# A drain instruction in GpSimd's stream at the start of the last gate pair

## The chip, the cores and the metric

The kernel runs on one core of a Trainium2 chip. The metric is the device time of one execution in microseconds (us), as the median over runs. Beside the timed runs there is one profiled execution, from which every duration below is read.

## The reference, cut to what matters

One layer of a streaming encoder trunk is computed for 2048 prompt frames and 32 sample frames of width 1024:

```python
def layer(h, p, conv_hist, pool_hist, pos, g_mix, w_in, conv_w, conv_b, pool_w, pool_scale,
          w_out, g_ple, w_ple_gate, w_ple):
    hn = rmsnorm(h, g_mix)
    proj = hn @ w_in
    ...
    h = h + jnp.concatenate([yA, yB], axis=-1) @ w_out
    gate = jax.nn.sigmoid(rmsnorm(h, g_ple) @ w_ple_gate)
    h = h + (p @ w_ple) * gate
    return h, new_conv, new_pool
```

After it a last RMSNorm with `g_final` is applied: `y = h * rsqrt(mean(h*h) + EPS) * g_final`. The change lies in the last stage, which computes the gate, the sum `h + (p @ w_ple) * gate` and the last RMSNorm.

## The kernel before, in words

Frames stand in tiles of 128; there are 16 tiles for the prompt (0 to 15) and a short one for the sample. The last stage takes the prompt's tiles in pairs (0 and 1, 2 and 3, up to 14 and 15). A pair's product with the gate weight is made of seven smaller products (`seven`), each of 12 matmuls, that add into three PSUM banks `x`, `y` and `z`. What comes out of a bank goes to `carry` (a copy by ScalarE) or to `out`.

For all pairs but the last, `out` and `done_g` finish a tile: the sigmoid on ScalarE, two VectorE operations (`L1584`, `L1585`), the sum of squares on ScalarE (`L94`, into `ssq_f`), then two operations of one column on GpSimd, `L73` (`ms_f`, mean and epsilon) and `L77` (`rstd_f`, the power -0.5), then VectorE's `L1592`, which multiplies the tile by `rstd_f` and `g_final`, and the DMA `L1593` that writes the tile out. From tile 6 on this DMA is issued by SyncE; for earlier tiles by GpSimd.

The last pair, tiles 14 and 15, is `last_pair`. It is called with a function `before` that finishes tile 13 in the middle of the pair (after the third of the seven products), by `done_g(13)`. Tile 12 has been finished by `done_g(12)` just ahead of the call. In `last_pair` the names are:

- `L1670`: VectorE adds what a PSUM bank holds to the carried half (`c_g`); `L1666`: ScalarE's sigmoid of it.
- `L1633` and `L1634` (`gated`): VectorE multiplies by the embedding product (`e`, or `e_l` from PSUM) and adds to `h`.
- `L1638` (`square`): ScalarE's sum of squares of a half; `L1641` and `L1643`: GpSimd adds the parts up; `L1650` (`root`): GpSimd's power -0.5 of the sum.
- `L1646` (`weigh`): the product with `g_final`, once on GpSimd (for the first half of tile 14), otherwise on VectorE.
- `L1657`, `L1659` (`normed`): VectorE and ScalarE multiply by the root, and the DMAs at `L1658` and `L1660` write out.
- `L1715`: the last product of the pair, in two halves of 256 columns, that adds into bank `x` after `L1670` has read it; `L109`: TensorE's embedding products `e_l`.

Every engine works its own instructions off in the order in which they stand. A scheduler places the instructions by dependencies and priorities; those marked by `fixed` (`keep_in_program_order`) stand where the program has them.

DMAs are issued from three places: SyncE (SP), ScalarE (ACT) and GpSimd (POOL). GpSimd issues 148 DMAs in all; the last are the writes of early tiles at `L1593`. At the kernel's end each engine has a drain instruction and all engines meet twice at a barrier, which GpSimd leads: it waits until the four others have arrived, then releases them. These instructions bear the line `L1845`, that of the kernel's call, and those at the start `L1836`.

Of the kernel before, what the change touches and what calls it, by code (L numbers as in the profile page):

```python
# [36 lines left out]
def trunk(ctx, tc, x_p, x_s, c_conv, c_pool, p_p, p_s, g_mix, w_in, conv_w, conv_b, pool_w,  # L37
          pool_scale, w_out, g_ple, w_gate, w_ple, g_fin, y_p, y_s, sc_p, sp_p, sc_s, sp_s):
    nc = tc.nc
# [16 lines left out]
    def bank(name):  # L56
        return ps_m.tile([P, 512], F32, tag="mm", name=name)
# [48 lines left out]
    def embed_product(ps, pps, wp, cs):  # L106
        for k in range(2):
            for q, (a, b) in enumerate(((0, 0), (0, 1), (1, 0))):
                nc.tensor.matmul(ps, pps[:, a, k], wp[k][b][:, cs], start=k + q == 0, stop=k == 1 and q == 2)  # L109
# [1194 lines left out]
    with ExitStack() as s2:  # L1304
# [308 lines left out]
        def last_pair(i, A, before):  # L1613
# [15 lines left out]
            fixed = lambda ins: tc.keep_in_program_order(ins)  # L1629
# [51 lines left out]
            def of_first(cs, eng):  # L1681
                square(0, cs)
                weigh(0, cs, eng)
# [8 lines left out]
            def rest():  # L1692
                of_first(cols_of(0), nc.gpsimd)

            def second(cols):

                ps = bank(f"e_l{cols.start}")[:, :cols.stop - cols.start]
                embed_product(ps, pps, wp, cols)
                return ps

            def upper_half():
                gated(1, cols_of(1), at_last["gate"], second(cols_of(1)))

            def end(X):

                t = st.tile([P, NH], F32, tag="t", name="g_l")
                m = NH // 2  # L1710
                cs = [slice(o, o + m) for o in (0, m)]
                for c, part in enumerate(cs):
                    for k in range(KH):
                        for a, b in FINE:
                            nc.tensor.matmul(X[:, part], A["22"][:, k, a], W["T4"][b][:, k, part], start=False,  # L1715
                                             stop=k == KH - 1 and (a, b) == FINE[-1], skip_group_check=True)
                    fixed(sigmoid(t[:, part], X[:, part], 1))
                    ee = second(part)
                    if c == 0:
                        normed(0, at_last["root"])  # L1720
                        square(1, cols_of(1))
                    gated(1, part, t[:, part], ee)
                    if c == 0:
                        weigh(1, cols_of(1))
                for part in cs:
                    square(1, part)
                weigh(1, cols_of(0))
                normed(1, root(1))
# [80 lines left out]
        for i in range(0, NT - 3, 2):  # L1809
# [8 lines left out]
            if i + 2 < NT - 3:  # L1818
                done_g(i + 1, h[1])
        last_pair(NT - 3, S[NT - 3], lambda: done_g(NT - 4, h[1], True))  # L1820

# [27 lines left out]
```

## Time and profile before

| what | us |
| --- | --- |
| median of the runs | 916.7 |
| runs | 914.71, 917.25, 916.7 |
| the profiled execution's own time | 913.25 |
| its span, from first to last instruction | 911.5 |

The profile's page gives the busy time of each engine: PE is TensorE's matmuls, PEld its weight loads, DVE is VectorE, ACT ScalarE, POOL GpSimd and SP SyncE. A letter q behind an engine's name is its sequencer: drains, semaphore waits and DMA issues are told of under that name and are not counted as busy. In a timeline the columns are the start in us, the duration in us, then engine, line, operation, the tile written and the tiles read, shape and count; in brackets stands the idle time of the engine ahead of it, and what ended it. The answer for one source line gives, for each kind of instruction of it, the count, the shortest, median and longest duration in ns, and the first and last start in us.

### The profile page before, as it was taken

The numbers are of one execution on the slowest core, as the hardware profiler recorded it, in microseconds if no ns is written. First come the engines' busy times: TensorE is split into PE (matmuls) and PEld (weight loads), VectorE is DVE, ScalarE is ACT, GpSimd is POOL, SyncE is SP. The second block draws the span as 40 slices with busy tenths as digits, with TensorE's granted clock in tenths as the row PEclk, the third lists the DMA queues.
The fourth block names the chain that finished last, engine by engine and source line by source line (L and its number), as shares of the span: only waits on it lengthen the run. The fifth ranks groups of instructions, "written<-read, shape, count | busy, mean of one in ns | idle before, by whom it ended". The sixth has DMA issues, their size and how long they took to land.

```text
span 911.5 us, 12171 instructions
## 1 busy us (share of the span) xinstructions
PE 894.6 (98%) x4174; PEld 722.5 (79%) x4174; DVE 702.9 (77%) x1158; ACT 460.6 (51%) x834; POOL 149.8 (16%) x290
## 2 busy tenths in 40 slices
PE   8999999999999999999999999999999999999996
PEld 6788888878888887877778887888788888778885
DVE  6899789797993697846667579965666988897885
ACT  7744555455443345533344366544434865565554
POOL 2210121222122114100000020121111211120012
PEclk9999999999999999999999999999999999999999
DMA  8255296748599767567746495887777975575554
GB/s 268 61 187 179 76 269 191 217 151 262 151 328 422 212 201 216 199 216 236 256 129 199 162 318 200 260 245 257 212 267 256 325 257 174 184 237 185 184 192 167
DMA packets 113387, 198.52 MB, mean 218 GB/s; under 512 B 13174, under 2 KB 70062, under 8 KB 112429
## 3 DMA queue, kind: packets, MB, share of 16 engines
q1 hardware_dynamic: 91309, 124.72, 42.5%
q0 software_dynamic: 19568, 68.62, 22.5%
q10 hardware_dynamic: 2448, 4.39, 1.3%
q8 instruction: 33, 0.54, 0.2%
q14 instruction: 29, 0.24, 0.1%
HBM read 132.53 MB, written 65.15 MB: 217 GB/s over the span
## 4 chain that ended last, share of the span: by engine, by line
PE 54%; issue 11%; DMA 10%; DVE 2%; POOL 1%; ACT 1%; POOLq 0%; ACTq 0%; DVEq 0%
PE x_g L185 9%; PE x_o L185 7%; PE z_g L185 5%; DMA raw_zab_0b<-in_w_in_dram 4%; PE x_zab L646 4%; PE x_zbv L646 3%; PE z_o L185 3%; PE x_ch L646 3%; PE y_g L185 2%; PE z_zab L646 2%; PE y_o L185 2%; DMA B<-p_d 2%; PE e L109 2%; PE z_ch L646 1%; PE z_zbv L646 1%
## 5 line engine op out<-in xcount | busy, mean ns | idle before, releaser
L185 PE MATMUL z_o<-wo,y_S 128*128 128x512 f32 x192 | 47.4, 389 | 0.0
L646 PE MATMUL x_zab<-B,w_zab_S 128*128 128x512 f32 x192 | 46.9, 393 | 0.4 <-DVE w_zab_S L84 0.2
L185 PE MATMUL x_o<-wo_T,y_S 128*128 128x512 f32 x192 | 46.3, 390 | 0.6 <-DVE c_o L1319 0.6
L185 PE MATMUL z_g<-wg,g_S 128*128 128x512 f32 x192 | 46.8, 391 | 0.0
L646 PE MATMUL z_zab<-B,w_zab_S 128*128 128x512 f32 x192 | 46.7, 391 | 0.0
L185 PE MATMUL x_o<-wo,y 128*128 128x512 f32 x192 | 45.2, 389 | 0.0
L646 PEld LDWEIGHTS x_zab<-B,w_zab_S 128*128 128x128 f32 x192 | 35.7, 188 | 9.4 <-DVE w_zab_S L84 0.6
L185 PEld LDWEIGHTS x_o<-wo_T,y_S 128*128 128x128 f32 x192 | 35.9, 188 | 8.4 <-DVE c_o L1319 1.0
L185 PEld LDWEIGHTS x_o<-wo,y 128*128 128x128 f32 x192 | 36.1, 188 | 7.7
L646 PEld LDWEIGHTS z_zab<-B,w_zab_S 128*128 128x128 f32 x192 | 35.8, 188 | 7.8 <-DVE w_zab_S L84 0.3
L185 PEld LDWEIGHTS z_o<-wo,y_S 128*128 128x128 f32 x192 | 36.1, 188 | 7.5
L646 PE MATMUL x_ch<-B,w_ch_S 128*128 128x512 f32 x168 | 41.9, 392 | 0.0
L185 PEld LDWEIGHTS z_g<-wg,g_S 128*128 128x128 f32 x192 | 35.8, 188 | 7.5 <-ACT c_g L1573 0.2
L646 PE MATMUL z_ch<-B,w_ch_S 128*128 128x512 f32 x168 | 40.5, 390 | 1.1 <-ACT U L986 1.1
L646 PE MATMUL x_zbv<-B,w_zbv_S 128*128 128x512 f32 x168 | 40.9, 392 | 0.3 <-ACT zs L986 0.3
L646 PE MATMUL z_zbv<-B,w_zbv_S 128*128 128x512 f32 x168 | 40.4, 390 | 0.0
L646 PEld LDWEIGHTS z_ch<-B,w_ch_S 128*128 128x128 f32 x168 | 31.5, 188 | 8.1 <-ACT U L986 1.6
L646 PEld LDWEIGHTS x_zbv<-B,w_zbv_S 128*128 128x128 f32 x168 | 31.3, 188 | 8.1 <-ACT zs L986 0.8
L646 PEld LDWEIGHTS x_ch<-B,w_ch_S 128*128 128x128 f32 x168 | 31.3, 188 | 7.3 <-ACT U L986 0.4
L646 PEld LDWEIGHTS z_zbv<-B,w_zbv_S 128*128 128x128 f32 x168 | 31.5, 188 | 6.5
L81 ACT CAST y_S<-y_fS 128x512 fp32r<-128x512 f32 x28 | 17.0, 619 | 28.1 <-PE x_o L185 12.2
L1319 DVE TENSOR_TENSOR c_o<-x_o,x 128x512 f32<-128x512 f32 x14 | 9.7, 689 | 22.6 <-PE x_o L185 22.6
(552 smaller groups left out, 2285.0 us busy)
## 6 DMA issues: line engine op xcount, KB each, us to landing
wn<-in_w_in_dram SPq DMA_DIRECT2D x24, 512.0 KB, 4.7
y<-y_d SPq DMA_DIRECT2D x16, 512.0 KB, 6.5
p_dT<-T POOLq DMA_DIRECT2D x15, 512.0 KB, 5.2
e<-e_d SPq DMA_DIRECT2D x15, 512.0 KB, 5.0
x<-in_x_prompt_dram SPq DMA_DIRECT2D x14, 512.0 KB, 4.9
B<-p_d POOLq DMA_DIRECT2D x3, 2048.0 KB, 16.8
B<-p_dT POOLq DMA_DIRECT2D x3, 2048.0 KB, 22.8
h_d<-x SPq DMA_DIRECT2D x12, 512.0 KB, 6.3
```

Of the source, the lines that this page charges most:

```text
L81: ins = nc.scalar.copy(hi, src)
L109: nc.tensor.matmul(ps, pps[:, a, k], wp[k][b][:, cs], start=k + q == 0, stop=k == 1 and q == 2)
L185: nc.tensor.matmul(ps[:n], lhs[:, k, a, :n], w[b][:, k], start=start and k + q == 0, stop=k == KH - 1 and q == 2, skip_group_check=True)
L646: nc.tensor.matmul(ps, lhs[:, k, x], b[:, k, y], start=start and k + q == 0, stop=stop and k == KH - 1 and q == 2, skip_group_check=True)
L1319: add = lambda o, a, b: nc.vector.tensor_tensor(o, a, b, op=ALU.add)
```

## The change

One instruction is added: a drain in GpSimd's stream, in the function `last_pair`, fixed to its place in the program. It writes nothing, waits for no semaphore and raises none. No DMA is issued by GpSimd after this place.

```diff
             def rest():
                 of_first(cols_of(0), nc.gpsimd)
 
+            fixed(nc.gpsimd.drain())
+
             def second(cols):
 
                 ps = bank(f"e_l{cols.start}")[:, :cols.stop - cols.start]
```

In the built program the drain stands between `L77` of tile 12 (`rstd_f`) and `L73` of tile 13 (`ms_f`). GpSimd's instructions are otherwise the same ones in the same order, with the same waits; so are those of all the other engines. Lines behind the change move down by two, so that the kernel's end bears `L1847` in the changed kernel.

## The prediction

> **What bounds the kernel now.** I read the page first, then the chain of waits of the last 20 us, then the drains at the kernel's end, and last the timelines of the engines around the place of the new instruction.
>
> ```profile
> span 911.5 us, 12171 instructions
> PE 894.6 (98%) x4174; PEld 722.5 (79%) x4174; DVE 702.9 (77%) x1158; ACT 460.6 (51%) x834; POOL 149.8 (16%) x290
> ```
>
> TensorE is busy in 98% of the span and GpSimd in 16%. An instruction on GpSimd costs nothing unless somebody waits for it, so the case is decided in the last stretch, where small operations on all engines follow one another. The chain that ended last, in order of time (start, duration, what):
>
> ```profile
> 901.49 1.55 PE x_g L1715 x12
> 903.04 0.73 PE e_l L109 x6
> ...
> 905.32 0.02 POOLq L1643
> 905.34 0.09 issue
> 905.43 0.19 POOL ssq_l L1643
> 905.62 0.04 issue
> 905.66 0.61 POOLq L1845
> 906.27 0.02 issue
> 906.30 0.61 ACT hg L1659
> ```
>
> TensorE sets the time up to about 903.8; then come sum, square, root and scaling of the last tile, until 906.9. The row POOLq L1845 at 905.66 is no compute: it is GpSimd's sequencer entering the drain of the kernel's end. The drains and barrier at that end, and GpSimd's drain at the start of the program:
>
> ```profile
> L1845 POOLq EVENT_SEMAPHORE  x4: 17/17/17, 910.7 to 911.4; - x4
> L1845 POOLq DRAIN  x3: 46/98/5027, 905.7 to 911.2; - x3
> L1845 SPq DRAIN  x3: 7/7/7, 910.0 to 911.0; - x3
> L1836 POOLq DRAIN  x1: 169/169/169, 0.3 to 0.3; - x1
> ```
>
> Of GpSimd's three drains at the end one takes 5.03 us, the two behind it 0.10 and 0.05; the one at the start, ahead of any DMA, took 0.17. The long one begins at 905.66 and ends at 910.69. SyncE arrives at the barrier at 910.0, after the last output has landed; GpSimd, which leads the barrier, goes on at 910.7. So the end waits about 0.7 us for GpSimd's drain alone, and only that much of its 5.03 us is on the path.
>
> **The change part by part.** First the price of the new drain. GpSimd's operations around its place, and its last one:
>
> ```profile
> 888.54 0.74 POOL L73 TENSOR_SCALAR ms_f<-ssq_f 128x1 f32<-128x1 f32 x1 [16.70 <-ACT junk L94]
> 889.37 0.55 POOL L77 TENSOR_TENSOR rstd_f<-ms_f,nhalf 128x1 f32<-128x1 f32 x1
> 891.55 0.19 POOL L73 TENSOR_SCALAR ms_f<-ssq_f 128x1 f32<-128x1 f32 x1 [1.63 <-ACT junk L94]
> 891.82 0.55 POOL L77 TENSOR_TENSOR rstd_f<-ms_f,nhalf 128x1 f32<-128x1 f32 x1
> 895.99 0.23 POOL L1641 TENSOR_SCALAR ssq_l<-ssq_l 128x1 f32<-128x1 f32 x1 [3.63 <-ACT junk L1638]
> 896.31 1.31 POOL L1646 TENSOR_TENSOR hg<-h,g_bc 128x512 f32<-128x512 f32 x1
> ...
> 905.70 0.57 POOL L1650 TENSOR_TENSOR rstd_l<-ssq_l,nhalf 128x1 f32<-128x1 f32 x1
> ```
>
> At the end GpSimd's last operation is over at 905.70 + 0.57 = 906.27, and the drain lasts until 910.69: 4.42 us beyond the idle engine. The trace does not say what fills them. Three of the four drains stand where GpSimd has issued no DMA since the last drain, and they take 0.05 to 0.17 us; the long one is the first behind all of its DMAs. Those had been issued long before:
>
> ```profile
> L1593 POOL DMA_DIRECT2D out_dram<-h x7: 531/606/611, 758.1 to 811.9; - x7
> ```
>
> The last issue is at 811.9, 94 us ahead of the long drain and 77 us ahead of the new one, so both find the same history. I take it that the price is owed once for the DMAs issued since the last drain, whenever the drain comes. The new drain's price beyond idle is then bounded by 0.05 us below and 5.03 above (the whole row, if none of it ran beside the last operation); I take 4.42, from the row with the same DMAs behind it. By the same reading the drain at the end falls to about 0.1 us.
>
> There is a rule against this. The Trainium skill, "PSUM — Partial Sum Buffer", section "Engine vs sequencer instructions", says that a drain waits for the engine to go fully idle. Taken as the whole of it, the long drain would have ended at 906.27; the trace has 910.69, so it waits for something more.
>
> Now what stands behind it. The drain begins beyond L77 of tile 12, at 889.37 + 0.55 = 889.92. GpSimd then sits idle for 1.63 us until ScalarE's sum for tile 13 lets L73 start at 891.55: so much is covered. With 4.42 us the drain ends at 894.34; L73 follows at about 894.45, L77 0.27 later (as in the rows) at 894.72, ending at 895.27. Queued behind the drain on GpSimd are these two, then L1641 and L1646; the one who waits is VectorE:
>
> ```profile
> 892.40 1.28 DVE L1592 SCALAR_TENSOR_TENSOR h<-h,rstd_f,g_bc 128x1024 f32<-128x1024 f32 x1 [0.57 <-POOL rstd_f L77]
> 893.60 0.69 DVE L1633 TENSOR_TENSOR c_g<-e,c_g 128x512 f32<-128x512 f32 x1
> 894.32 0.69 DVE L1634 TENSOR_TENSOR h<-h,c_g 128x512 f32<-128x512 f32 x1
> 896.20 0.69 DVE L1670 TENSOR_TENSOR c_g<-z_g,c_g 128x512 f32<-128x512 f32 x1 [1.18 <-PE z_g L185]
> 897.68 0.69 DVE L1633 TENSOR_TENSOR c_g<-e,c_g 128x512 f32<-128x512 f32 x1 [0.79 <-ACT c_g L1666]
> 898.29 0.68 DVE L1670 TENSOR_TENSOR c_g<-x_g,c_g 128x512 f32<-128x512 f32 x1
> ```
>
> L1592 of tile 13 moves from 892.40 to 895.30, 2.90 late. VectorE's order is fixed, so L1633 comes at 896.50, L1634 at 897.22, and L1670 on z_g at 897.94 instead of 896.20. Here 1.18 us of idle time, the wait for TensorE, is used up; 1.74 us are left. ScalarE stands next:
>
> ```profile
> 895.18 0.63 ACT L1638 ACTIVATE junk<-h 128x512 bf16<-128x512 f32 x1 [2.11 <-DVE h L1634]
> 895.72 0.19 ACT L1638 ACTIVATION_READ_ACCUMULATOR junk<-h 128x1 f32 x1
> 896.92 0.72 ACT L1666 ACTIVATE c_g<-c_g,rs_h 128x512 f32<-128x512 f32 x1 [1.01 <-DVE c_g L1670]
> ```
>
> Its square L1638 follows L1634 (end 895.01, start 895.18) and so moves to 898.08; its last piece, 0.54 us behind it and 0.19 long, ends at 898.81. L1666, which before waited for L1670 alone, now starts at about 898.82 instead of 896.92: 1.90 late. From it VectorE's L1633 comes at 899.58 and L1670 on x_g at 900.19, still 1.90 late, and L1670 frees the bank for TensorE:
>
> ```profile
> 897.81 1.52 PE L109 MATMUL e_l<-wl,pps_l 128*128 128x512 f32 x6
> 899.17 1.60 PE L1715 MATMUL x_g<-wq,g 128*128 128x256 f32 x12
> ```
>
> L1715 started at 899.17, right behind the end of L1670 at 898.97, while e_l was just ending. There is no slack, and L1715 moves by 1.90 us, and with it everything in the chain shown above. SyncE's issue for tile 13 goes 2.9 us late too; its next ones wait for the scaled tile 14, far down the same chain, so nothing queues behind it. TensorE's other products and all other instructions are unchanged.
>
> The sum: 1.90 us late into the tail, 0.7 us saved at the barrier since GpSimd no longer arrives after SyncE: +1.2 us. Against the profiled execution's 913.25 that is 914.45; the runs' median is 916.7, 3.45 above that execution, and I carry the difference over to it: 917.9. A difference under 0.3% (2.75 us) is about what a measurement of this kernel can tell from none, so my forecast is a loss that will hardly be seen.
>
> In general, with d for the drain's time beyond idle, the loss is d - 2.52 (none below that; 4.42 - 1.90 = 2.52 is covered), and 0.7 comes back if the drain at the end becomes short. If both drains cost the same d, loss and gain nearly cancel: a longer d adds to both.
>
> **The rivals.**
>
> *The new drain is cheap here and the one at the end gets short.* If it takes less than 2.52 us, all of it is hidden: 0.7 us faster, 916.0. For it: the other three drains take 0.05 to 0.17. Against: they have no DMAs behind them.
>
> *It does not do what it is there for.* If a drain costs only its engine's idle time here, and the 5.03 us belong to the kernel's end (the last outputs landing, the other engines), nothing changes: 916.7. This is where the skill's rule named above would lead for the new drain. Against: outputs have landed when SyncE arrives at 910.0, and GpSimd's drain lasts 0.7 us longer.
>
> *The price is not paid off.* Both drains take 4.42 us: the loss of 1.90 us stays, and as the end moves with it, nothing comes back: 918.6. For it: the two short drains at the end follow within 0.3 us and have no operation ahead of them, so they do not prove a payment.
>
> *A collision on SBUF.* With the delay, GpSimd's L1641 starts at 898.90, and L1646 0.31 later at 899.21, until 900.52; VectorE's L1633, which reads two SBUF operands, wants to start at 899.58. Before, L1646 ended at 897.62, just ahead of L1633 at 897.68. That the two hinder each other is seen in the other direction: L73 took 0.74 us at 888.54, and 0.19 at 891.55; beside the slow one ran
>
> ```profile
> 888.55 0.68 DVE L1585 TENSOR_TENSOR h<-h,e 128x512 f32<-128x512 f32 x1
> ```
>
> which ended at 889.23, and L73 at 889.28. If VectorE is held in turn, L1633 starts at 900.52, 0.94 us later still: +2.1 us, 918.8. The Trainium skill, "SBUF — State Buffer", section "SBUF: two separate sides", has this as a rule: a VectorE operation with two SBUF inputs and a GpSimd operation that reads SBUF exclude each other, and whichever starts first holds the port for its whole instruction. The rows above agree for GpSimd being held; none shows VectorE held.
>
> *The drain costs more in the middle than at the end: slower.* At 889 SyncE's loads and stores run beside it; at the end hardly any do. How much traffic can stretch a small transfer is seen in the writes at L1593:
>
> ```profile
> DMA to landing us min/median/max: 2.3/3.6/5.4
> ```
>
> Longest over median is 1.5. If whatever the drain waits for stretches so, d is 6.63, the loss 4.11, less 0.7: +3.4 us, 920.1. It decides from d = 5.97 on (2.52 + 0.7 + 2.75). Against: some 3 us of the long drain at the end (906.9 to 910.0) also pass beside transfers, those of the last outputs.
>
> **How the numbers follow.** Chances: the forecast 0.40, hidden 0.12, no effect 0.08, not paid off 0.09, collision 0.14, dearer in the middle 0.15, and 0.02 for what I do not see. The predicted time is that of the likeliest, 917.9. The range goes from 915.2 (the hidden case, 916.0, with 0.8 us for the scatter of a median of runs that lie between 914.71 and 917.25) to 920.1 (the dearer drain); beyond it is part of that last case and some scatter, under 2 in 10. Slower by over 0.3% is the dearer drain, and 0.04 of the collision, which is 0.6 us short of the bound: 0.19. Faster by over 0.3% has no mechanism, since only 0.7 us can be saved; 0.04 for the hidden case with scatter and the unseen. The rest, 0.77, lies within 0.3%.
>
> **What would show it.** In the changed kernel's trace: a GpSimd drain at line 1695 that begins near 889.4 and ends near 894.3; L73 of tile 13 near 894.4; L1592 near 895.3 with over 3 us idle ahead of it; L1715 1.9 us later against the start of the last pair; the first drain of the end about 0.1 us beyond the last L1650, and the barrier's release following SyncE's arrival directly. I am wrong if the new drain is under 2.5 us, if the one at the end still lasts 4 us beyond idle, or if L1633 starts only when L1646 has ended.

## The result

The changed kernel takes 917.46 us against 915.42 us for the kernel before, as medians of 20 runs each. The ratio is 1.0025 with an interval of 1.0016 to 1.0034, so the drain makes the kernel slower by 2.3 us (1.5 to 3.1); the two medians lie 2.0 us apart. The interval excludes no change and reaches just over the 0.3% that the prediction took as the least that can be told. (The prediction was made with a median of 916.7 for the kernel before, from three of these 20 runs.)

In the changed kernel's profile the drain and the end stand as follows (answers for lines 1695 and 1847):

```profile
L1695 POOLq DRAIN  x1: 5012/5012/5012, 891.3 to 891.3; - x1
```

```profile
L1847 POOLq EVENT_SEMAPHORE  x4: 17/17/17, 914.7 to 915.3; - x4
L1847 POOLq DRAIN  x3: 34/97/677, 910.3 to 915.1; - x3
L1847 SPq DRAIN  x3: 7/7/7, 914.6 to 914.9; - x3
L1847 ACTq DRAIN  x2: 8/80/152, 912.0 to 914.9; - x2
```

The new drain lasts 5.01 us. The longest at the end, 5.03 us before, is down to 0.68, of which 0.57 lie beside the last operation. SyncE arrives at 914.6 and the barrier goes on at 914.7: the 0.7 us of waiting for GpSimd are gone. The timelines of GpSimd, VectorE, ScalarE and TensorE behind the drain:

```profile
891.38 0.55 POOL L77 TENSOR_TENSOR rstd_f<-ms_f,nhalf 128x1 f32<-128x1 f32 x1
896.47 0.19 POOL L73 TENSOR_SCALAR ms_f<-ssq_f 128x1 f32<-128x1 f32 x1 [4.54 <-issue]
896.74 0.55 POOL L77 TENSOR_TENSOR rstd_f<-ms_f,nhalf 128x1 f32<-128x1 f32 x1
...
901.23 1.26 POOL L1646 TENSOR_TENSOR hg<-h,g_bc 128x512 f32<-128x512 f32 x1
```

```profile
897.32 1.28 DVE L1592 SCALAR_TENSOR_TENSOR h<-h,rstd_f,g_bc 128x1024 f32<-128x1024 f32 x1 [3.47 <-POOL rstd_f L77]
...
901.47 1.56 DVE L1633 TENSOR_TENSOR c_g<-e,c_g 128x512 f32<-128x512 f32 x1 [0.94 <-ACT c_g L1666]
902.96 0.68 DVE L1670 TENSOR_TENSOR c_g<-x_g,c_g 128x512 f32<-128x512 f32 x1
```

```profile
900.73 0.71 ACT L1666 ACTIVATE c_g<-c_g,rs_h 128x512 f32<-128x512 f32 x1
...
903.69 1.70 PE L1717 MATMUL x_g<-wq,g 128*128 128x256 f32 x12 [2.38 <-DVE c_g L1670]
```

This execution was already 2.01 us later than the one before when it reached the root of tile 12 (L77 at 891.38 against 889.37), in a part of the program that is the same; so everything is read from that root. L73 of tile 13 comes 5.09 us behind it (2.18 before), L1592 5.94 (3.03), L1666 9.35 (7.55). Then L1633 lasts 1.56 us where it took 0.69, L1670 starts at 11.58 (8.92), and TensorE's last product at 12.31 (9.80), now with 2.38 us of idle time ahead of it. From the root to the end of the span are 24.0 us (915.4 less 891.38) against 22.1: 1.9 us more, inside the interval of the runs.

### The profile page after: what moved, and what is told of

It is laid out like the page before. It is cut to its first block, busy times and chain, and to the rows that moved or that the text cites. A ratio compares the mean times of both kernels' runs of the same rounds, so it can differ in the third digit from the quotient of the medians.

```text
span 915.4 us, 12172 instructions
## 1 busy us (share of the span) xinstructions
PE 895.7 (98%) x4174; PEld 722.5 (79%) x4174; DVE 703.5 (77%) x1158; ACT 460.7 (50%) x834; POOL 149.9 (16%) x290
## 5 line engine op out<-in xcount | busy, mean ns | idle before, releaser
L1592 DVE SCALAR_TENSOR_TENSOR h<-h,rstd_f,g_bc 128x1024 f32<-128x1024 f32 (+1 forms) x15 | 19.2, 1280 | 12.1 <-POOL rstd_f L77 12.0
```

The costliest lines, as they stand in the source:

```text
L1592: nc.vector.scalar_tensor_tensor(h[:n], h[:n], rf[:n], g_bc[:n], op0=ALU.mult, op1=ALU.mult)
```

## The experiments

Two questions were open: whether the drain's price is a debt for GpSimd's DMAs, paid once, and whether GpSimd's L1646 really holds VectorE. Each kernel is read from the root of tile 12 to the end of its span, 22.1 us in the kernel before and 24.0 in the changed one, since the runs alone scatter by more than the terms in question. The trace of each kernel is one execution; the kernel with the two operations exchanged and no drain, read below, gives the 22.1 a second time.

**The drain where nobody waits.**

```diff
             if i + 2 < NT - 3:
                 done_g(i + 1, h[1])
+            if i == 10:
+                tc.keep_in_program_order(nc.gpsimd.drain())
```

> The drain is moved to an earlier place, behind L77 of tile 11, where all of GpSimd's DMAs have been issued too and GpSimd then sits idle for 16.7 us. Theory A (a debt: the first drain behind GpSimd's DMAs pays about 4.4 us beyond idle, once): the new drain lasts about 5.0 us near 871, nobody waits for it, the first drain at the end lasts under 0.8 us and ends with the last operation, and the barrier waits for SyncE alone: 0.7 us faster than before, ratio about 0.9992. Rival B (every first drain after a long time costs 4.4 us): the new one 5.0 us, the one at the end 5.0 us again, no change. Rival C (the 5 us belong to the kernel's end): the new one under 0.7 us, the end 5.0 us, no change.

The drain, the operation before it and the next one:

```profile
L1821 POOLq DRAIN  x1: 5338/5338/5338, 873.3 to 873.3; - x1
```

```profile
873.34 0.88 POOL L77 TENSOR_TENSOR rstd_f<-ms_f,nhalf 128x1 f32<-128x1 f32 x1
890.88 0.74 POOL L73 TENSOR_SCALAR ms_f<-ssq_f 128x1 f32<-128x1 f32 x1 [16.66 <-ACT junk L94]
891.70 0.55 POOL L77 TENSOR_TENSOR rstd_f<-ms_f,nhalf 128x1 f32<-128x1 f32 x1
```

```profile
L1847 POOLq DRAIN  x3: 34/98/677, 908.0 to 912.9; - x3
```

Beyond the last operation (873.34 + 0.88 = 874.22) the drain lasts until 878.64, again 4.42 us, and the next operation waits for ScalarE as before. The end's drain is short. From the root of tile 12 to the end are 913.1 - 891.70 = 21.4 us, 0.7 less than before. The ratio is 0.9992 (0.9977 to 1.0007): the expected value, but not to be told from no change by the runs. Theory A holds in the trace, B and C are out.

**The collision taken away, the drain kept.**

```diff
             def rest():
-                of_first(cols_of(0), nc.gpsimd)
+                weigh(0, cols_of(0), nc.gpsimd)
+                square(0, cols_of(0))
```

> The changed kernel, with GpSimd's two operations for the first half of tile 14 in the other order: the product with g_final (L1646 in the kernel before) ahead of the small sum (L1641), so that it starts when L1634 ends instead of 1.3 us later, and is over before VectorE's next L1633 starts. Collision theory: that L1633 lasts 0.69 us instead of 1.56, TensorE's last product comes about 0.9 us earlier than in the changed kernel, the loss against before falls from 2.3 to about 1.2 us, ratio about 1.0013. Rival (the 1.56 us have another cause, for instance the later place in time): it stays at 1.56, ratio 1.0025.

GpSimd, VectorE and TensorE in this kernel:

```profile
889.39 0.55 POOL L77 TENSOR_TENSOR rstd_f<-ms_f,nhalf 128x1 f32<-128x1 f32 x1
...
898.02 1.29 POOL L1646 TENSOR_TENSOR hg<-h,g_bc 128x512 f32<-128x512 f32 x1 [2.73 <-DVE h L1634]
```

```profile
899.49 0.69 DVE L1633 TENSOR_TENSOR c_g<-e,c_g 128x512 f32<-128x512 f32 x1 [0.94 <-ACT c_g L1666]
900.10 0.68 DVE L1670 TENSOR_TENSOR c_g<-x_g,c_g 128x512 f32<-128x512 f32 x1
```

```profile
900.83 1.70 PE L1718 MATMUL x_g<-wq,g 128*128 128x256 f32 x12 [1.50 <-DVE c_g L1670]
```

L1646 is over at 899.31, ahead of L1633, which is back at 0.69 us. The root of tile 12 is at 889.39 here, so L1670 starts 10.71 us behind it (11.58 with the collision) and TensorE's product 11.44 (12.31): 0.87 us earlier. From the root to the end are 912.5 - 889.39 = 23.1 us, 1.0 more than before and 0.9 less than in the changed kernel. The ratio against before is 1.0004 (0.9990 to 1.0019), too wide to settle this alone; the reading rests on the trace.

**The exchange by itself.** The edit is the same, on the kernel before.

> The kernel before, without the drain, with the same two GpSimd operations exchanged. In the kernel before the two do not collide, so both theories expect no change in time (ratio 1.000, within 0.001); it shows whether the exchange by itself gains or costs anything, which has to be known to read the run beside it. GpSimd's product should start near 895.1 instead of 896.3 and last 1.3 us.

```profile
890.63 0.55 POOL L77 TENSOR_TENSOR rstd_f<-ms_f,nhalf 128x1 f32<-128x1 f32 x1
...
896.38 1.30 POOL L1646 TENSOR_TENSOR hg<-h,g_bc 128x512 f32<-128x512 f32 x1 [2.73 <-DVE h L1634]
```

The root of tile 12 was at 890.63 in this run, 1.26 later than in the profile before, so 896.38 is the expected 895.1. To the end are 912.7 - 890.63 = 22.1 us, as before, and the ratio is 1.0000 (0.9986 to 1.0015). The exchange is neutral where nothing collides.

**The collision without a drain.**

```diff
             def rest():
-                of_first(cols_of(0), nc.gpsimd)
+                square(0, cols_of(0))
+                for c in range(2):
+                    t = sm.tile([P, 1], F32, tag="ms", name=f"delay_{c}")
+                    fixed(nc.gpsimd.tensor_tensor(t, g_bc[:, :1], nhalf, op=ALU.pow))
+                weigh(0, cols_of(0), nc.gpsimd)
```

> The kernel before, without the drain, with two one-column powers (0.55 us each, results unused) put between GpSimd's L1641 and L1646 of tile 14, so that L1646 runs from about 897.5 to 898.8 and overlaps VectorE's L1633 of 897.68. Collision theory: that L1633 is held and ends within 0.1 us of the end of L1646, 0.5 to 0.9 us later than in before, TensorE's last product moves by as much, and the kernel gets 0.4 to 0.9 us slower with no drain in it, ratio about 1.0007. Rival (GpSimd is the one that is held): L1633 keeps 0.69 us, L1646 takes over 1.6 us, no change in time.

```profile
889.59 0.55 POOL L77 TENSOR_TENSOR rstd_f<-ms_f,nhalf 128x1 f32<-128x1 f32 x1
...
897.57 1.29 POOL L1646 TENSOR_TENSOR hg<-h,g_bc 128x512 f32<-128x512 f32 x1
```

```profile
897.89 1.51 DVE L1633 TENSOR_TENSOR c_g<-e,c_g 128x512 f32<-128x512 f32 x1 [0.79 <-ACT c_g L1666]
899.33 0.68 DVE L1670 TENSOR_TENSOR c_g<-x_g,c_g 128x512 f32<-128x512 f32 x1
```

```profile
900.06 1.69 PE L1719 MATMUL x_g<-wq,g 128*128 128x256 f32 x12 [0.51 <-DVE c_g L1670]
```

L1646 keeps its 1.3 us and L1633 takes 1.51 instead of 0.69: it is VectorE that is held. It ends at 899.40, 0.54 behind the end of L1646 at 898.86; I had expected within 0.1. About half a microsecond of the operation thus comes behind the end of L1646. From the root at 889.59 the product starts at 10.47 (9.80 before), and to the end are 912.5 - 889.59 = 22.9 us, 0.8 more than before. The ratio is 1.0006 (0.9993 to 1.0020), again not settled by the runs.

**How the price is made up.** Drains at more places, all results from one execution each:

```diff
+    tc.keep_in_program_order(nc.gpsimd.drain())
     def rstd_of(ssq, n, name, r=None):
...
         S, W = {}, {}
+        tc.keep_in_program_order(nc.gpsimd.drain())
         with tc.issue_after(last_raw):
...
+        tc.keep_in_program_order(nc.gpsimd.drain())
         W = {}
         tops, _ = rows_of_weight(ya, "wg_t", g_d, 0)
...
                 done_g(i + 1, h[1])
+            if i == 10:
+                tc.keep_in_program_order(nc.gpsimd.drain())
```

> The kernel before with four more drains on GpSimd: ahead of any of its DMAs, behind 98 of them, behind 28 further ones, and behind the last 22 (at the place behind tile 11). If the price is a debt of so much for each DMA since the last drain, 4.42 us for 148 is 0.030 us each: the first costs under 0.2 us, the last 0.66 us beyond idle, the one behind 28 about 0.84 and the one behind 98 about 2.9, the middle two more if DMAs are still on their way; the end's first drain under 0.1 beyond its last operation. If the price is fixed, each of the three behind DMAs costs about 4.4 us. If it goes by bytes or packets and not by DMAs, the three stand to each other as those do.

The drain behind 98 DMAs, the one behind 28 more, the one behind the last 22 and the operation ahead of that:

```profile
L1396 POOLq DRAIN  x1: 10657/10657/10657, 530.7 to 530.7; - x1
```

```profile
L1506 POOLq DRAIN  x1: 6854/6854/6854, 715.8 to 715.8; - x1
```

```profile
L1825 POOLq DRAIN  x1: 2789/2789/2789, 876.3 to 876.3; - x1
```

```profile
876.37 0.88 POOL L79 TENSOR_TENSOR rstd_f<-ms_f,nhalf 128x1 f32<-128x1 f32 x1
```

The last one ends at 879.12, 1.87 us beyond the operation (877.25): neither 0.66 nor 4.4. The other two stand right behind DMAs that had just been issued, and took longer than any price above; how much of them is waiting for those to land these runs do not part. The one ahead of all DMAs took 0.28 us in all, 0.08 beyond the operation beside it, and the first one at the end 0.08 beyond its last operation, as expected; behind DMAs neither a share of 0.030 us each nor a fixed price holds. So three more kernels followed, each with the drain behind tile 11 and one further drain, at these places in turn:

```diff
             if gi == 1:
+                tc.keep_in_program_order(nc.gpsimd.drain())
...
         S, W = {}, {}
+        tc.keep_in_program_order(nc.gpsimd.drain())
         with tc.issue_after(last_raw):
...
             done_g(i, h[0])
+            if i == 2:
+                tc.keep_in_program_order(nc.gpsimd.drain())
             if i in (0, 2, 4):
```

> The drain behind tile 11 as in the first run, and one more in the first stage, so that 110 DMAs lie between the two. So far 148 cost 4.42 us beyond idle and 22 cost 1.87. If the price is a fixed part and so much for each DMA (1.42 us and 0.0202 us each, from these two), it is 3.65 us here. If it is so much for each DMA (1.87 / 22 = 0.085 us) up to a limit of 52, it is 4.42.

> The same with the further drain ahead of the second stage, so that 50 DMAs lie between. Fixed part and so much each: 2.43 us beyond idle behind tile 11. So much each up to a limit: 4.25.

> The same with the further drain in the last stage, so that 5 DMAs lie between, all of them landed 50 us before. Fixed part and so much each: 1.52 us beyond idle. So much each up to a limit: 0.43.

The drain behind tile 11 and the operation ahead of it, in the order of these three:

```profile
L1822 POOLq DRAIN  x1: 5410/5410/5410, 882.6 to 882.6; - x1
```

```profile
882.60 0.88 POOL L77 TENSOR_TENSOR rstd_f<-ms_f,nhalf 128x1 f32<-128x1 f32 x1
```

```profile
L1822 POOLq DRAIN  x1: 5084/5084/5084, 875.6 to 875.6; - x1
```

```profile
875.68 0.88 POOL L77 TENSOR_TENSOR rstd_f<-ms_f,nhalf 128x1 f32<-128x1 f32 x1
```

```profile
L1823 POOLq DRAIN  x1: 1404/1404/1404, 875.9 to 875.9; - x1
```

```profile
875.90 0.88 POOL L77 TENSOR_TENSOR rstd_f<-ms_f,nhalf 128x1 f32<-128x1 f32 x1
```

Beyond the operation (the drain enters 0.04 us ahead of it and the operation takes 0.88) that is 4.49 us behind 110 DMAs, 4.17 behind 50 and 0.49 behind 5. With 1.87 behind 22 and 4.42 behind 148, the price is about 0.085 us for each DMA since the last drain, up to a limit near 4.4 us, which somewhat over 50 of them reach. The law with a fixed part is out: it gives 2.43 for 50 and 1.52 for 5. Why there is a limit these runs do not show.

Whether the price goes by bytes or packets instead can be read from the same traces. The 5, 22 and 50 DMAs of GpSimd move 2.2, 10.7 and 21.2 MB in 624, 2976 and 9056 packets. The first drain at the end, with no DMA since the one behind tile 11, takes 0.07 to 0.08 us beyond the last operation. Less that, the price is 0.08 us for each DMA in all three, 0.17 to 0.19 us for each MB, and 0.45 to 0.66 ns for each packet. The count fits best, bytes less well and packets badly; but count, bytes and the time since the last drain all grow together here, and no run holds one of them fixed.

The kernel with 110 also took 923.97 us against 915.22 in its one run. Its other drain stands in the first stage, right behind fresh DMAs, and lasts 7 us:

```profile
L1291 POOLq DRAIN  x1: 7043/7043/7043, 261.1 to 261.1; - x1
```

GpSimd's loads of `B` (`L560`) start only behind this drain, at 268.70, and at 277.94 TensorE has been idle for 2.92 us until one of them landed; VectorE's work falls 6.0 us further behind that of the kernel before between 254 and 281 us. The other three kernels with further drains took 918.0, 916.98 and 917.54 us in one run each, against 915.0 to 915.2 for the kernel before beside them; single runs do not settle such differences.

**The drain one root later.**

```diff
-        last_pair(NT - 3, S[NT - 3], lambda: done_g(NT - 4, h[1], True))
+        last_pair(NT - 3, S[NT - 3], lambda: (done_g(NT - 4, h[1], True), tc.keep_in_program_order(nc.gpsimd.drain())))
```

> The drain behind L77 of tile 13, one root later than in the changed kernel, where GpSimd idles for 3.6 us. With 4.4 us beyond idle it ends about 0.8 us after L1641 wants to start (896.8 against 896.0). L1592 of tile 13 is not delayed at all, so L1633 and L1670 start as before. GpSimd's L1646 runs from about 897.2 to 898.5, and by the collision theory VectorE's L1633 of 897.68 is held until about 898.5, which ends 0.8 us later than before; TensorE's last product moves by about that, 0.7 us come back at the barrier, in all about +0.1 us. Without a collision L1633 keeps 0.69 us and the end comes 0.7 us earlier.

```profile
L1820 POOLq DRAIN  x1: 5010/5010/5010, 893.4 to 893.4; - x1
```

```profile
891.03 0.55 POOL L77 TENSOR_TENSOR rstd_f<-ms_f,nhalf 128x1 f32<-128x1 f32 x1
...
898.88 1.30 POOL L1646 TENSOR_TENSOR hg<-h,g_bc 128x512 f32<-128x512 f32 x1
```

```profile
899.35 1.39 DVE L1633 TENSOR_TENSOR c_g<-e,c_g 128x512 f32<-128x512 f32 x1 [0.79 <-ACT c_g L1666]
```

No root is delayed here, and still L1633 is held: 1.39 us, ending 0.56 behind the end of L1646 (900.18). From the root of tile 12 (891.03) to the end are 913.1 - 891.03 = 22.0 us (22.1 before), where 0.1 more was expected: the delay of about 0.6 and the 0.7 saved cancel.

## Why the prediction came out as it did

The time lies in the range, 915.2 to 920.1, and the loss is of the forecast's sign, but larger: 2.3 us by the runs and 1.9 by the traces, against 1.2. That 917.46 is so near to the 917.9 forecast is luck: the median of three runs from which the forecast started was 1.3 us above that of all 20, and the loss was forecast about 1 us too small.

- The drain's price, 4.42 us beyond idle, was right to 0.01 us, and it did not depend on the place: 4.42 at 874, at 892 and at 906. The rival of a dearer drain in the middle is out; so are those of a cheap drain, of no effect and of a price not paid off, since the first drain at the end lasts only 0.07 us beyond its last operation. That the price belongs to GpSimd's DMAs and is paid once was right in kind; that the whole of 148 DMAs is owed was not: somewhat over 50 suffice.
- The 0.7 us at the barrier came back, as worked out: in the traces of the changed kernel and of the three others with one added drain (behind tile 11, with the exchange, one root later) the barrier goes on within 0.04 us of SyncE's arrival, against 0.7 before.
- The delay down to L1666 was nearly right: 1.80 us late in the changed kernel (9.35 against 7.55), where 1.90 stood. One smaller step was wrong: "There is no slack". In the kernel before, L1715 starts 0.20 us behind the end of L1670; where L1670 comes late, with or without the collision, it starts 0.05 behind, so about 0.15 us were slack. Without the collision the product is therefore 1.64 us late instead of 1.90, and the loss to the end is 1.0 us, where the sum gave 1.2.
- The step that failed is the one from L1666 to L1670: "VectorE's L1633 comes at 899.58 and L1670 on x_g at 900.19, still 1.90 late". L1633 came when expected and then took 1.56 us instead of 0.69, because GpSimd's L1646 had been pushed into it. This was the rival of the collision, priced at 0.94 us and given 0.14; it cost 0.87. With the 1.0 us that the delay costs by itself it makes the 1.9 us of the trace. The prediction named as a sign of being wrong that L1633 starts only when L1646 has ended; the trace shows the same wait in another form, as a start on time and a longer duration. I had both rows that collide, with their times 0.4 us apart, and held the rival at a low chance since the trace before shows only GpSimd being held. Three kernels show VectorE held, for 1.39 to 1.56 us, and one with the overlap taken away shows 0.69. The rule of the Trainium skill ("SBUF — State Buffer", section "SBUF: two separate sides") is that two such operations exclude each other, whichever starts first. The three traces agree: L1646 started 0.24 to 0.47 us ahead of L1633 and kept its 1.3 us. One row of the trace before bears on the operands: L1670 at 896.20, which reads one operand from PSUM, ran beside L1646, and neither was stretched (0.69 and 1.31 us). Beyond that the runs vary only the overlap; that it is a port which the two share, none of them shows.
- The rule of the Trainium skill that a drain waits for the engine to go fully idle ("PSUM — Partial Sum Buffer", section "Engine vs sequencer instructions") was rightly not taken as the whole price. In these traces GpSimd's drain lasts up to 4.5 us beyond that, even where its DMAs had landed 50 us before.

The version that does better than both in the trace is the drain behind tile 11, 0.7 us shorter than before; the interval of its ratio, 0.9977 to 1.0007, includes 1, so the runs do not show a gain.

## What to carry to other kernels

GpSimd's drain behind its own DMAs has a price that shows only in the profile's sequencer rows. It is not one of every engine that issues DMAs: SyncE issues 339 here and its drains take 0.007 us, ScalarE 17 and its longest takes 0.15. Find the long drain at the kernel's end, see how much of it the last barrier really waits for, and if it is to be paid earlier, put it where that engine's next instruction waits longer than the price, and where none of its DMAs waits to be issued behind it. When a change delays one engine's work, lay the delayed operations beside all that then run at the same time, not only beside those that wait for them: here a product on an almost idle engine, harmless at its old time, held another engine at its new one and cost nearly as much as the delay itself.

## What the runs showed of the hardware that was not expected

Beyond the operation ahead of it GpSimd's drain took about 0.085 us for each of its DMAs since the last drain, 50 us and more after they had landed, and no more than about 4.5 us in all: 0.49 for 5, 1.87 for 22, 4.17 for 50, 4.49 for 110 and 4.42 for 148. A VectorE operation with two operands in SBUF that is held by GpSimd's product of 128x512 does not start late in the profile: it starts on time and its duration grows, from 0.69 to as much as 1.56 us, and it ends some 0.55 us behind the GpSimd operation.
